# Layer 1 inputs in the order q, z, kv; S4, scaled tables and the second sequence's turned x1 through DRAM

## The chip, the core and the metric

The kernel runs on one core of a Trainium2 chip. The metric is the device time of one execution in microseconds (us). The core's engines work side by side, each through its own list of instructions in order: PE (TensorE) multiplies matrices into PSUM banks, DVE (VectorE), ACT (ScalarE) and POOL (GpSimd) work on elements, and SP (SyncE) issues nearly all DMA transfers, one after the other. An instruction that waits holds up all that stand behind it on its engine.

## What is computed

Two sequences, p of 1024 tokens and s of 512, run through two layers of width 1024. Layer 0 mixes by pooling and a gated recurrence; layer 1 is attention with eight query heads, two key/value heads, RMS norm and rotary positions (rope) on q and k, and a gate from z:

```python
def odd_mixer(x, w_in, q_norm_g, k_norm_g, w_out):
    proj = x @ w_in
    q, k, v, z = jnp.split(proj, IN1_SPLIT_POINTS, axis=-1)
    q = rms_norm(q.reshape(B, T, ATTN_HEADS, HEAD_DIM), q_norm_g)
    k = rms_norm(k.reshape(B, T, KV_HEADS, HEAD_DIM), k_norm_g)
    ...
    q = apply_axial_rope(q, cos, sin)
    k = apply_axial_rope(k, cos, sin)
    o = blocked_attention(q, k, v)
    return (o * jax.nn.silu(z)) @ w_out

for layer in range(DEPTH):
    ...
    x = layer_norm(ALPHA * x + mix, ln_g[layer], ln_b[layer])
```

## The kernel before

**Numbers.** Every matrix operand is split into a high part (`h`, rounded to the matmul type) and a low part (`l`, what is left); a product is three matmuls: high x high, low x high, high x low. ACT or POOL makes the high part (L88, L85), DVE the low part (L91). A `unit` is a 128x512 block of weights: one load, one high, one low.

**Stages.** Layer 0's projections run to about 170 us, its heads to 620, its output and the layer norm ("mid") to 752. `layer1_in` then makes the inputs of layer 1 until 1119, and attention and output follow. In mid, `mid_pair` turns the rows of x1 for p on PE and makes the six operands A11, A12, A22, S1, S2, S3 from them.

**The products of p.** `PRODUCTS` names seven products that replace eight block products, in the order P1 (A11), P2 (A12), P6 (S2), P5 (S1), P3 (S4), P7 (S3), P4 (A22). S4 = A12 - S2 is a seventh operand, which `last_sum` makes after P2 of kv, from the split parts: sum, sum, difference, high, low (L975 to L977). The sums of weights that the products need are made in layer 0 by `weight_sums`, a generator that the projections advance (two steps per group), and stored to DRAM. `gathered` adds each product's bank on DVE (L1094) to tiles u2 and u4 or to one of two c tiles; a finished block goes to `finish`, which is `kv_done`, `q_done` or, in `z_pair`, the gate. Only then is the bank free; there are five banks, `mm` (two) and `me` (three), used in turn. A kv tile takes 12 matmuls of 256 columns per bank, a q or z tile 12 of 512.

**Order.** For p: kv, z, q. `feed` lists the units in this order, and `next_units` keeps up to eight prepared ahead. The first eight are made during mid, in tiles of their own. Then comes s: its four blocks of x1 are loaded, turned (L903), split and used for kv (`kvs`), q (`qs`) and z; its units come from `wunit`, high part on POOL. A scheduler orders the instructions of each engine from the program's order and its own estimates of durations.

**Rope.** `rope` takes squares on ACT (L996), a small op on DVE (L997), pow on POOL (L999), the product with the cos table (L1001, on POOL for p, on DVE for s), one product with the sin table per head on DVE (L1006), and the add on POOL (L1007). For q a further DVE op (L1155) scales the result of pow into `rq`; for k the result scales the rows on DVE (L1137). PE turns the rows (L1159 for q, into Tqp or Tqs; L1138 for k, into kTkp or kTks), ACT copies q out of PSUM, and a DMA stores it to qd. `rope_consts` loads cos, sin and the gains and multiplies the tables on DVE (L1016), anew for k of p, q of p and both of s.

Of the kernel before, what the change touches and what calls it, by code (L numbers as in the profile page):

```python
# [56 lines left out]
class Kern:  # L57
    def __init__(self, ctx, tc, a):
# [906 lines left out]
    def last_sum(self):  # L965

        nc = self.nc
        tags = [f"x{p}{k}0" for k in range(4) for p in "hl"]
        at = {"h": tags[0::2], "l": tags[1::2]}
        parts = {x: [self.x0p.tile([P, 512], F32R, tag=t, name=f"S4{x}{k}") for k, t in enumerate(at[x])] for x in "hl"}  # L970
        for k in range(4):
            (ah, al), (sh, sl) = (tuple(x[k // 2][:, k % 2, :] for x in self.A[b]) for b in ("A12", "S2"))
            a, b = self.raw(f"s4a{k}"), self.raw(f"s4b{k}")
            add = nc.gpsimd if k % 2 else nc.vector
            add.tensor_tensor(out=a, in0=ah.bitcast(F32), in1=al.bitcast(F32), op=ALU.add)  # L975
# [13 lines left out]
    def rope(self, ps, nh, n, tabs, t1, t2, name, mul):  # L989
# [7 lines left out]
        nc.vector.tensor_scalar(ss[:, 0:nh], ss[:, 0:nh], 1.0 / DH, RMS_EPS, ALU.mult, ALU.add)  # L997
# [1 line left out]
        nc.gpsimd.tensor_tensor(out=rs[:, 0:nh], in0=ss[:, 0:nh], in1=self.mhalf[:, 0:nh], op=ALU.pow)  # L999
# [1 line left out]
        mul.tensor_tensor(out=t1[:, 0:W].rearrange("p (h f) -> p h f", f=P), in0=ps.rearrange("p (h f) -> p h f", f=P),  # L1001
                                in1=ct[:, n:n + 1, :].to_broadcast([P, nh, P]), op=ALU.mult)
# [566 lines left out]
```

## Time and profile before

| what | us |
|---|---|
| three runs | 1573.17, 1573.67, 1574.72 |
| median | 1573.67 |
| the profiled execution, its own time | 1565.18 |
| its span in the trace | 1563.2 |

The span is what the trace covers; the views count from its start. The profiled execution is a run of its own, 8.5 us under the median of the other three. In the prediction's fences a group row reads: line, engine, operation, output and inputs by the program's names, shapes, count | busy us, mean ns of one | idle time before them and who ended it.

### The profile page before, as it was taken

How to read it: one execution, taken by the hardware profiler on the slowest of the kernel's cores; microseconds unless marked ns; L12 is line 12 of the kernel's file. 1: busy time of each engine (PE TensorE's matmuls, PEld its weight loads, DVE VectorE, ACT ScalarE, POOL GpSimd, SP SyncE). 2: the span in 40 equal slices, each digit the busy share in tenths (PEclk: the TensorE clock that was granted, in tenths of full speed). 3: DMA queues.
4: the chain of work that ended last, by engine and by line, in shares of the span. 5: the costliest groups of instructions: out<-in, count | busy, mean ns of one | idle time of the engine just before them, and what ended most of it. 6: DMA issues, size and time to landing. Idle time of an engine off the chain costs nothing.

```text
span 1563.2 us, 21698 instructions
## 1 busy us (share of the span) xinstructions
PE 1474.5 (94%) x7214; PEld 1211.3 (77%) x7214; DVE 1077.7 (69%) x2062; ACT 722.2 (46%) x1628; POOL 727.9 (47%) x726
## 2 busy tenths in 40 slices
PE   9989998989987989999889999899999999999997
PEld 7767886878776778778778877677778888888786
DVE  5672256587767978868795378766577777777775
ACT  3222354555554655345244343412675555555651
POOL 5441244254375563539740046855444444544642
PEclk9999999999997999999999999999999999999999
DMA  9962343234535646544435444444340111111211
GB/s 329 371 219 64 116 115 90 92 109 127 158 106 162 189 149 196 162 136 156 135 120 173 140 161 122 112 125 142 108 148 28 55 54 55 55 49 60 80 63 54
DMA packets 150144, 198.58 MB, mean 127 GB/s; under 512 B 12032, under 2 KB 77824, under 8 KB 150032
## 3 DMA queue, kind: packets, MB, share of 16 engines
q1 hardware_dynamic: 150032, 197.19, 39.8%
q8 instruction: 57, 0.93, 0.3%
q14 instruction: 55, 0.45, 0.1%
HBM read 139.43 MB, written 57.72 MB: 126 GB/s over the span
## 4 chain that ended last, share of the span: by engine, by line
PE 59%; DVE 20%; DMA 9%; ACT 4%; issue 4%; POOL 2%; SPq 1%; DVEq 0%; ACTq 0%; POOLq 0%
PE Sp L98 6%; PE Op L98 5%; PE o1p L98 5%; PE tp L98 4%; PE ptp L1357 3%; PE o1s L98 3%; PE o0p L98 3%; PE zp L98 3%; PE qs L98 3%; PE ts L98 2%; PE z L98 2%; DVE t1qp L1006 1%; PE o0s L98 1%; PE Ss L98 1%; PE z4P L98 1%
## 5 line engine op out<-in xcount | busy, mean ns | idle before, releaser
L1335 POOL TENSOR_SCALAR prp<-prp,smp 128x1024 f32<-128x1024 f32 x64 | 72.6, 1134 | 124.7 <-DVE smp L1334 114.1
L88 ACT CAST pwp<-ptp 128x512 fp32r<-128x512 f32 x128 | 74.8, 584 | 95.8 <-PE ptp L1357 95.6
L98 PE MATMUL Op<-pwp,Vhp 128*128 128x512 f32 x256 | 108.9, 425 | 0.0
L91 DVE TENSOR_TENSOR pwp<-ptp,pwp 128x512 fp32r<-128x512 f32 x128 | 87.1, 682 | 21.3 <-ACT pwp L88 21.3
L1330 ACT ACTIVATE prp<-Sp,nbp,rqp 128x1024 f32<-128x1024 f32 (+1 forms) x68 | 78.7, 1158 | 20.5 <-DVE nbp L1327 14.0
L1322 DVE TENSOR_REDUCE nbp<-Sp 128x1 f32<-128x1024 f32 (+1 forms) x68 | 78.3, 1153 | 9.7 <-PE Sp L98 9.7
L1357 PE MATMUL ptp<-idn,prp 128*128 128x128 f32 x512 | 77.4, 273 | 4.1 <-ACT zs L1260 3.2
L1357 PEld LDWEIGHTS ptp<-idn,prp 128*128 128x128 f32 x512 | 64.0, 141 | 22.2 <-POOL prp L1335 4.7
L1001 POOL TENSOR_TENSOR t0qp<-cq,rt0qp 128x512 f32<-128x512 f32 x8 | 10.7, 1339 | 107.9 <-DVE cq L1094 100.5
L98 PEld LDWEIGHTS Op<-pwp,Vhp 128*128 128x128 f32 x256 | 48.3, 189 | 7.0
L98 PE MATMUL o0p<-wo0h,ah0p 128*128 128x512 f32 x128 | 51.1, 400 | 0.4 <-ACT wo0h L88 0.4
L98 PE MATMUL o0p<-wo0l,ah0p 128*128 128x512 f32 x128 | 51.0, 400 | 0.0
L98 PE MATMUL o0p<-wo0h,al0p 128*128 128x512 f32 x128 | 50.9, 398 | 0.0
L98 PE MATMUL tp<-wt_l,xhp 128*128 128x512 f32 x128 | 50.3, 397 | 0.0
L98 PE MATMUL tp<-wt_h,xlp 128*128 128x512 f32 x128 | 50.3, 396 | 0.0
L98 PE MATMUL Op<-pwp,Vlp 128*128 128x512 f32 x128 | 50.1, 391 | 0.0
L98 PE MATMUL tp<-wt_h,xhp 128*128 128x512 f32 x128 | 49.8, 402 | 0.0
L658 DVE SCALAR_TENSOR_TENSOR Usp<-Usp,decbp 128x130 f32<-128x130 f32 x48 | 23.7, 495 | 27.7 <-ACT Usp L623 27.2
L98 PE MATMUL Sp<-Khp,qhp 128*128 128x512 f32 x128 | 42.4, 408 | 0.0
L1335 POOL TENSOR_SCALAR prs<-prs,sms 128x512 f32<-128x512 f32 x32 | 24.3, 761 | 36.1 <-DVE sms L1334 23.8
L98 PE MATMUL Sp<-Klp,qhp 128*128 128x512 f32 x128 | 41.0, 396 | 0.0
L98 PE MATMUL Sp<-Khp,qlp 128*128 128x512 f32 x128 | 40.8, 395 | 0.0
(1181 smaller groups left out, 5251.3 us busy)
## 6 DMA issues: line engine op xcount, KB each, us to landing
wt_r<-w0t SPq DMA_DIRECT2D x16, 256.0 KB, 4.1
xrp<-xT_p SPq DMA_DIRECT2D x16, 256.0 KB, 5.1
srq<-w1q SPq DMA_DIRECT2D x16, 256.0 KB, 5.4
xrs<-xT_s SPq DMA_DIRECT2D x16, 256.0 KB, 5.1
sum_q<-srq SPq DMA_DIRECT2D x16, 256.0 KB, 5.1
srz<-w1z SPq DMA_DIRECT2D x16, 256.0 KB, 4.2
sum_z<-srz SPq DMA_DIRECT2D x16, 256.0 KB, 2.3
wp<-rd_p SPq DMA_DIRECT2D x16, 256.0 KB, 5.3
```

The source lines that it names most:

```text
L88: self.nc.scalar.copy(out, in_)
L91: self.nc.vector.tensor_tensor(out=out, in0=in_, in1=hi.bitcast(F32), op=ALU.subtract)
L98: self.nc.tensor.matmul(out, lhsT=lhsT, rhs=rhs, start=start, stop=stop)
L658: nc.vector.scalar_tensor_tensor(out=U[:, i, :], in0=U[:, i + o, :], scalar=dec[:, 4 * d + h, n:n + 1], in1=U[:, i, :], op0=ALU.mult, op1= ...
L1001: mul.tensor_tensor(out=t1[:, 0:W].rearrange("p (h f) -> p h f", f=P), in0=ps.rearrange("p (h f) -> p h f", f=P), in1=ct[:, n:n + 1, :].to ...
L1006: nc.vector.tensor_tensor(out=v(t2[:, c]), in0=v(ps[:, c])[:, :, ::-1, :], in1=v(st[:, n, :]), op=ALU.mult)
L1322: nc.vector.tensor_reduce(out=nb[:, i:i + 1], in_=b, op=ALU.max, axis=AX.X, negate=True)
L1330: nc.scalar.activation(pr[:, i * W:(i + 1) * W], b, AF.Exp, bias=nb[:, 0:1], scale=rq, accum_out=sm[:, i:i + 1])
L1335: nc.gpsimd.tensor_scalar(pr, pr, sm, 0.0, ALU.mult, ALU.add)
L1357: nc.tensor.transpose(pt[:, h * P:(h + 1) * P], prs[h][:, c * P:(c + 1) * P], self.idn)
```

## The change

1. **Order.** For p the stages run q, z, kv. `feed` and `weight_sums` follow; the first eight units are those of P1 and P2 of q.
2. **S4.** `mid_pair` computes S4 in one DVE instruction from the unsplit S2 and the turned A12 and stores it to DRAM; `last_sum` loads it and splits it.
3. **Tables.** `weight_sums` ends with two more steps: cos and sin are multiplied with the four gains, once, and stored; `rope_tables` loads them.
4. **Rope.** The cos product is on DVE for p too; the sin product is two instructions for all heads; q's pow writes `rq` itself (the small op adds 128 times the epsilon, which includes the scale); k's scale moves from DVE to ACT.
5. **x1 of s.** After each of the four `z_pair`s `turn_second` loads one block of x1, turns and splits it, and stores the parts to DRAM; after P1 and after P2 of kv `load_second` loads one half of them back, into the tiles that A11 and A12 leave.
6. **High parts.** For the units of s (and half of the output's) they are made on ACT, no longer on POOL.
7. `z_pair` takes its sums from the u tiles in a rotation of four, not two.

```diff
+        s4 = hp.tile([P, 512], F32, tag="xbp", name=f"s4{i}", bufs=2)
+        nc.vector.scalar_tensor_tensor(out=s4, in0=s2, scalar=-1.0, in1=p12, op0=ALU.mult, op1=ALU.add)
+        self.load(self.s4d[:, :, c], v(s4))
...
-            add.tensor_tensor(out=a, in0=ah.bitcast(F32), in1=al.bitcast(F32), op=ALU.add)
-            add.tensor_tensor(out=b, in0=sh.bitcast(F32), in1=sl.bitcast(F32), op=ALU.add)
-            add.tensor_tensor(out=a, in0=a, in1=b, op=ALU.subtract)
+            raw = self.raw(f"s4{k}")
+            self.load(raw, self.s4d[:, k, :])
...
-        mul.tensor_tensor(out=t1[:, 0:W].rearrange("p (h f) -> p h f", f=P), in0=ps.rearrange("p (h f) -> p h f", f=P),
+        nc.vector.tensor_tensor(out=t1[:, 0:W].rearrange("p (h f) -> p h f", f=P), in0=ps.rearrange("p (h f) -> p h f", f=P),
                                 in1=ct[:, n:n + 1, :].to_broadcast([P, nh, P]), op=ALU.mult)
-        for h in range(nh):
-            c = slice(h * P, (h + 1) * P)
-            v = lambda x: x.rearrange("p (a b f) -> p a b f", b=2, f=32)
-            nc.vector.tensor_tensor(out=v(t2[:, c]), in0=v(ps[:, c])[:, :, ::-1, :], in1=v(st[:, n, :]), op=ALU.mult)
+        v = lambda x, b: x.rearrange("p (h a b f) -> p h a b f", a=2, b=2, f=32)[:, :, :, b, :]
+        for b in range(2):
+            nc.vector.tensor_tensor(out=v(t2[:, 0:W], b), in0=v(ps, 1 - b),
+                                    in1=v(st[:, n, :], b).to_broadcast([P, nh, 2, 32]), op=ALU.mult)
...
+        for h in range(2):
+            for i, n in enumerate(("cos", "sin")):
...
+                for w in range(2):
...
+                    nc.vector.tensor_tensor(out=o, in0=t, in1=g[:, 2 * w + i:2 * w + i + 1, :].to_broadcast([P, 4, P]), op=ALU.mult)
+                    self.load(self.tabd[w][i][:, ns, :], o)
...
-            nc.vector.tensor_scalar(t1[:, c], t1[:, c], rs[:, h:h + 1], None, ALU.mult)
+            nc.scalar.activation(t1[:, c], t1[:, c], AF.Copy, scale=rs[:, h:h + 1])
...
-        nc.vector.tensor_scalar(self.rq[s][:, n, 4 * piece:4 * piece + 4], rs, QK_SCALE, None, ALU.mult)
...
-        self.token_products("kv", 2, 256, u, kv_done, self.last_sum)
+        self.next_units(0)
         tabs = table(0, "qp")
+        self.token_products("q", 1, 512, u, q_done, lambda j: j == 1 and self.last_sum())
         for b in range(0, 8, 2):
             self.z_pair(b, u)
...
-        self.token_products("q", 1, 512, u, q_done)
+            self.turn_second(b // 2)
+        tabs = table(1, "kp")
+        self.token_products("kv", 2, 256, u, kv_done, lambda j: j < 2 and self.load_second(j))
...
+        self.hi_w = self.hi_act
...
+    def turn_second(self, i):
+
+        y = [self.tp.tile([P, 512], F32, tag="c", name=f"y1{i}{half}", bufs=2) for half in range(2)]
+        for half in range(2):
+            self.load(y[half], self.x1["s"][i][:, 512 * half:512 * half + 512])
+            pt = self.turned(y[half], 0, "mx", f"x1t{i}{half}")
+            h, l = (self.tp.tile([P, 512], F32R, tag="t", name=f"x1{x}{i}{half}", bufs=4) for x in "hl")
+            self.hi_act(h, pt)
+            self.lo_dve(l, pt, h)
+            for d, x in zip(self.x1t, (h, l)):
+                self.load(d[half][:, :, i * P:(i + 1) * P], x.bitcast(F32).rearrange("p (k t) -> p k t", t=P))
+
+    def load_second(self, half):
+        for j in (2 * half, 2 * half + 1):
+            for x, d, X in zip("hl", self.x1t, (self.XH, self.XL)):
+                X[2][j] = self.x1p.tile([P, 2, 512], F32R, tag=f"x1{x}2{j}", name=f"x1{x}2{j}")
+                self.load(X[2][j].bitcast(F32), d[half][:, 2 * (j % 2):2 * (j % 2) + 2, :])
```

How this moves the instructions is shown at three places; the scheduler decides them. Numbers behind names are tile numbers and differ between the kernels, as do line numbers (L1094 is L1109 after the change, L91 is L95, L1006 is L1011, L98 is L102).

First, DVE at the start of layer 1, from the first add that needs P2's bank. Before it is kv (ckv a c tile, kvP2i and kvP6i the banks, s4a and s4b the two sums for S4, rt0kp the cos table):

```order
L1094 TENSOR_TENSOR ckv_7818<-u_7721,kvP2i_7805 128x256
L1094 TENSOR_TENSOR ckv_7853<-u_7722,kvP2i_7840 128x256
L997 TENSOR_SCALAR sskp_7821<-sskp_7821 128x2
L1094 TENSOR_TENSOR u_7722<-u_7722,kvP6i_8007 128x256
L997 TENSOR_SCALAR sskp_7856<-sskp_7856 128x2
L975 TENSOR_TENSOR s4a_7953<-A12h_6723,A12l_6725 128x512
L976 TENSOR_TENSOR s4b_7954<-S2h_6727,S2l_6729 128x512
L1094 TENSOR_TENSOR u_7721<-u_7721,kvP6i_7993 128x256
L1016 TENSOR_TENSOR rt0kp<-rt0kp,rgkp 128x1024
L977 TENSOR_TENSOR s4a_7953<-s4a_7953,s4b_7954 128x512
L1016 TENSOR_TENSOR rt1kp<-rt1kp,rgkp 128x1024
```

After the change the same place is q (t0qp the cos product, t1qp the sin product, wlq the low part of a unit, S_ that of S4):

```order
L1109 TENSOR_TENSOR cq_7875<-u_7770,qP2i_7862 128x512
L1007 TENSOR_TENSOR t0qp_7877<-cq_7875,rt0qp 128x512
L1004 TENSOR_SCALAR ssqp_7879<-ssqp_7879 128x4
L1011 TENSOR_TENSOR t1qp_7878<-cq_7875,rt1qp 128x8x32 x2
L1109 TENSOR_TENSOR cq_7910<-u_7771,qP2i_7897 128x512
L95 TENSOR_TENSOR wlq_7839<-q0t_r,whq_7838 128x512
L1007 TENSOR_TENSOR t0qp_7912<-cq_7910,rt0qp 128x512
L95 TENSOR_TENSOR wlq_7845<-q1t_r,whq_7844 128x512
L95 TENSOR_TENSOR wlq_7851<-q2t_r,whq_7850 128x512
L1004 TENSOR_SCALAR ssqp_7914<-ssqp_7914 128x4
L1011 TENSOR_TENSOR t1qp_7913<-cq_7910,rt1qp 128x8x32 x2
L95 TENSOR_TENSOR wlq_7857<-q3t_r,whq_7856 128x512
```

The sums for S4 and the table products are gone from between the adds; the cos products have come in.

Second, DVE where P2 of kv now begins (kr are k's products with cos and sin):

```order
L1109 TENSOR_TENSOR ckv_9515<-u_7770,kvP2i_9502 128x256
L1007 TENSOR_TENSOR kr_9517<-ckv_9515,rt0kp 128x256
L1109 TENSOR_TENSOR ckv_9550<-u_7771,kvP2i_9537 128x256
L1001 TENSOR_SCALAR sskp_9518<-sskp_9518 128x2
L1011 TENSOR_TENSOR kr_9517<-ckv_9515,rt1kp 128x4x32 x2
L1007 TENSOR_TENSOR kr_9552<-ckv_9550,rt0kp 128x256
L1001 TENSOR_SCALAR sskp_9553<-sskp_9553 128x2
L1011 TENSOR_TENSOR kr_9552<-ckv_9550,rt1kp 128x4x32 x2
```

An add and its row's products now follow each other, and no scale of kr stands among them.

Third, PE where the keys and values of s begin. Before (x1t is a turned block of x1, kvs the bank, Tqp a turned row of q):

```order
L903 MATMUL x1t_10001<-idn,y_9999 128x128 x4
L1159 MATMUL Tqp_9697<-idn,t0qp_9680 128x128 x4
L98 MATMUL kvs_10136<-wkv_h,x1h_9991 128x512
L98 MATMUL kvs_10136<-wkv_l,x1h_9991 128x512
L1159 MATMUL Tqp_9736<-idn,t0qp_9719 128x128 x4
L98 MATMUL kvs_10136<-wkv_h,x1l_9995 128x512
```

and after, behind the last matmul of P4 of kv:

```order
L102 MATMUL kvP4i_10024<-whkv_9724,A22l_6779 128x256
L102 MATMUL kvs_10125<-wkv_h,x1h_9482 128x512
L102 MATMUL kvs_10125<-wkv_l,x1h_9482 128x512
L102 MATMUL kvs_10125<-wkv_h,x1l_9484 128x512
L102 MATMUL kvs_10125<-wkv_h,x1h_9482 128x512
```

The turns of x1 have gone to the z stage, and the rows of q that were still to be turned here have gone with q to the front.

More of the change, by code (lines that the diff above doesn't have):

```diff
@@ L309, in layer0 @@
                         if piece or gi:
-                            for _ in range(2):
+                            for _ in range(4 if piece and gi == len(groups) - 1 else 2):
                                 next(presums, None)
@@ L965, in last_sum @@
     def last_sum(self):
[L967 to L970, printed above, removed]
+        self.S4 = [], []
         for k in range(4):
[L972 to L975, printed above, removed]
-            add.tensor_tensor(out=b, in0=sh.bitcast(F32), in1=sl.bitcast(F32), op=ALU.add)
-            add.tensor_tensor(out=a, in0=a, in1=b, op=ALU.subtract)
-            self.hi_act(parts["h"][k], a)
-            self.lo_dve(parts["l"][k], a, parts["h"][k])
-        self.S4 = parts["h"], parts["l"]
+            h, l = (self.x0p.tile([P, 512], F32R, tag=f"x{'hl'[k % 2]}{2 * j + k // 2}0", name=f"S4{j}{k}") for j in range(2))
+            raw = self.raw(f"s4{k}")
+            self.load(raw, self.s4d[:, k, :])
+            self.hi_act(h, raw)
+            self.lo_dve(l, raw, h)
+            self.S4[0].append(h)
+            self.S4[1].append(l)
     def a_part(self, b, k):
@@ L1124, in token_products, with k_rows @@
                 self.gathered(prod, i, ps, u, W, finish, f"{name}{i}")
[L1125 to L1128 removed]
+            if after:
+                after(j)
+    def k_rows(self, s, g, i, src, tabs, t):
         nc = self.nc
@@ L1217, in layer1_in @@
         c4.close()
         tp = self.tp = ctx.enter_context(self.tc.tile_pool(name="t1p", bufs=1, reuse_waits="tile"))
-        tabs = [[t[:, 4 * w:4 * w + 4, :] for t in both] for both in [[tp.tile([P, 8, P], F32, tag=f"rt{i}", name=f"rts{i}") for i in range(2)]] for w in range(2)]
-        for w in range(2):
-            self.rope_consts(w, tp.tile([P, 2, P], F32, tag="rg", name=f"rgs{w}"), tabs[w], 4)
-        self.XH, self.XL = ({2: [self.x1p.tile([P, 2, 512], F32R, tag=f"x1{x}2{j}", name=f"x1{x}2{j}") for j in range(4)]} for x in "hl")
@@ L1224, in layer1_in @@
-        for i in range(4):
-            c = slice(i * P, (i + 1) * P)
-            y = self.x1p.tile([P, D], F32, tag=f"x1{'hl'[i % 2]}0{i // 2}", name=f"y1{i}")
-            self.load(y, self.x1[s][i])
-            for half in range(2):
-                pt = self.turned(y, half, "mx", f"x1t{i}{half}")
-                for j in range(2):
-                    xh, xl = (x[2][2 * half + j][:, :, c] for x in (self.XH, self.XL))
-                    pv = pt[:, 256 * j:256 * j + 256].rearrange("p (k t) -> p k t", t=P)
-                    self.hi_act(xh, pv)
-                    self.lo_dve(xl, pv, xh)
+        both = [tp.tile([P, 8, P], F32, tag=f"rt{i}", name=f"rts{i}") for i in range(2)]
@@ L1235, in layer1_in @@
+        tabs = [self.rope_tables(w, [t[:, 4 * w:4 * w + 4, :] for t in both], 4) for w in range(2)]
+        self.hi_w = self.hi_act
         self.kv_places(s, iter([f"x{x}{k}0" for k in range(4) for x in "hl"]))
```

68 lines of the change are left out of this document (37 added, 31 removed).

## The prediction

> **What bounds the kernel now.** First the page's head: which engine is nearly always busy.
>
> ```profile
> span 1563.2 us, 21698 instructions
> PE 1474.5 (94%) x7214; PEld 1211.3 (77%) x7214; DVE 1077.7 (69%) x2062; ACT 722.2 (46%) x1628; POOL 727.9 (47%) x726
> ```
>
> PE is busy for 94% of the span, but its ends are modelled, so "busy" hides stalls shorter than a matmul's modelled tail. The change touches the input of layer 1, so the second view is the table of windows over that stretch, cut where the chain of waits and the timeline show the parts to begin: keys/values of the first sequence (752), z (814), q (890), the second sequence's turning and keys/values (977), its q (1019), its z with the first scores (1072). The last row is this whole stretch.
>
> ```profile
> core 0: us, PE busy (x) PEld busy (x) DVE busy (x) ACT busy (x) POOL busy (x), PEclk, DMA share, GB/s
> 752.00:814.00 62.00, 49.81 (x359) 46.52 (x358) 52.26 (x109) 23.55 (x68) 32.42 (x30) 0.94 0.42 134
> 814.00:890.00 76.00, 76.00 (x334) 61.49 (x333) 44.18 (x82) 32.24 (x64) 7.05 (x9) 1.00 0.55 162
> 890.00:977.00 87.00, 83.82 (x373) 67.37 (x372) 60.96 (x114) 33.15 (x119) 39.28 (x33) 0.98 0.44 137
> 977.00:1019.00 42.00, 35.21 (x169) 27.46 (x167) 32.51 (x68) 19.23 (x82) 32.41 (x31) 0.92 0.45 125
> 1019.00:1072.00 53.00, 49.94 (x211) 38.84 (x210) 32.68 (x78) 9.99 (x53) 29.60 (x31) 0.94 0.35 103
> 1072.00:1120.00 48.00, 42.31 (x185) 33.67 (x184) 29.28 (x63) 27.38 (x67) 26.61 (x29) 0.96 0.54 162
> 752.00:1119.50 367.50, 336.58 (x1618) 274.85 (x1616) 251.68 (x510) 145.54 (x449) 167.08 (x161) 0.96 0.46 139
> ```
>
> Columns: stretch, its length, busy time of PE, weight load, DVE, ACT and POOL, the granted PE clock, DMA share and rate. In the z window PE has no idle time and full clock. In the first window it idles for 62.00 - 49.81 = 12.2 us, in 977:1019 for 6.8, in 1072:1120 for 5.7, and the clock is below one in just these windows. Over the stretch the idle time is 367.5 - 336.58 = 30.9 us; the clock loss, (1 - clock) x length added up over the six windows, is about 14 us.
>
> The third view, the chain of waits, gives PE's undisturbed pace and shows what starts the first window late.
>
> ```profile
> 765.55 5.59 DMA rt0kp<-cos
> ...
> 803.86 1.42 PE kvP4i L98 x12
> ...
> 850.86 19.53 PE z4P L98 x84
> ...
> 991.73 0.45 PE x1t L903 x4
> ```
>
> z4P: 84 matmuls of 512 columns in 19.53 us, 0.2325 us each. kvP4i: 12 of 256 columns in 1.42, 0.118 each. A group of four transposes: 0.45 at most. From these I make a floor for the stretch: kv of the first sequence 336 x 0.118 = 40; z and q 336 x 0.2325 = 78 each; the second sequence's kv 96, q 192, z 144 and 21 early score matmuls, 453 x 0.2325 = 105; some 38 groups of transposes, about 17. Together 319 of 367.5, so **about 48 us of excess**: 18 in 752:890 (138 - 40 - 78 - 2), 16 in 890:1019, 6 in 1019:1072, 8 after. That is all that the change can win here.
>
> The fourth view, PE's waits in these windows (engine, what waited, for whom: us, times, longest), names the causes.
>
> ```profile
> PE kvP5i L98 <- DVE ckv L1094: 3.6, 1, 3.6
> ...
> PE qP4i L98 <- DVE u L1094: 2.0, 1, 2.0
> PE Tqp L1159 <- POOL t0qp L1007: 1.2, 1, 1.2
> ...
> PE kvs L98 <- DVE x1l L91: 2.8, 3, 1.7
> PE x1t L903 <- DVE x1l L91: 2.1, 2, 2.0
> ...
> PE qs L98 <- POOL wq_h L85: 1.4, 1, 1.4
> ...
> PE ptp L1357 <- ACT zs L1260: 3.2, 1, 3.2
> ```
>
> The first window waits for DVE, which is late with the adds that empty the banks. The turn of the second sequence waits for its own low parts, one group after the other, and its kv for the last of them.
>
> **The change, part by part.** *The first window (order q, z, kv).* In the chain the tables land at 765.55 + 5.59 = 771.1 and must then be multiplied on DVE; DVE meanwhile forms S4. A kv bank lasts PE 12 x 0.118 = 1.4 us, five banks 7 us, so a DVE that is ten us late stops PE. A q bank lasts 12 x 0.2325 = 2.8 us, five banks 14 us. With q first, P2's third bank is full at 752 + 48 x 0.2325 + 3 x 2.8 = 771.6, and is wanted again by P6's third tile at 780. The tables, now only loaded, still stand behind the four stores of x_s on SP's queue, so they land near 771 again; P2's third add needs the c tile of the first row, some 6 us later (rope, turn, store): 777 against 780. P6's own four units stand behind the tables on SP, and PE wants them at 752 + 96 x 0.2325 = 774.3, just when they can be landed and split. I charge 1.5 us, bounded by 0 and by today's wait of 3.6 us for ckv.
>
> DVE's load decides whether q then keeps PE's pace.
>
> ```profile
> L1006 DVE TENSOR_TENSOR t1qp<-cq,rt1qp 128x128 f32<-128x128 f32 x32 | 15.9, 532 | 1.9 <-ACT t1qp L996 1.9
> L1006 DVE TENSOR_TENSOR krs<-kvs,rts 128x128 f32<-128x128 f32 x8 | 1.8, 277 | 0.0
> L1155 DVE TENSOR_SCALAR rqp<-rsqp 128x4 f32<-128x4 f32 x16 | 14.0, 877 | 3.5 <-POOL rsqp L999 3.5
> L997 DVE TENSOR_SCALAR ssqp<-ssqp 128x4 f32<-128x4 f32 x16 | 4.6, 289 | 0.0
> L1094 DVE TENSOR_TENSOR u<-u,qP7i 128x512 f32<-128x512 f32 x8 | 5.2, 674 | 0.0
> L1001 DVE TENSOR_TENSOR tqs<-qs,rts 128x512 f32<-128x512 f32 x8 | 5.5, 683 | 0.0
> L1001 DVE TENSOR_TENSOR krs<-kvs,rts 128x256 f32<-128x256 f32 x4 | 1.6, 414 | 0.0
> L91 DVE TENSOR_TENSOR wlq<-q2t_r,whq 128x512 fp32r<-128x512 f32 x4 | 2.7, 683 | 0.0
> ```
>
> Columns: line, engine, operation, tiles, shape, count | busy us, mean ns of one | idle before. A q row on DVE costs today 4 x 0.532 + 0.289 + 0.877 = 3.3 us. Afterwards: cos product 0.683 (the second sequence's row), two sin products of 128x256 at 0.414, the small scalar op 0.289, no scale: 1.8 us at the quiet price. But the first sequence's rope reads two tiles beside a busy POOL, and there the same sin product takes 532 ns instead of 277, a factor 1.92; the three products at that factor make 2.9 + 0.3 = 3.2 us. I take 2.5, half way, because POOL keeps pow and the add of a row but loses its cos product, 16 x 1.34 = 21 us:
>
> ```profile
> L1001 POOL TENSOR_TENSOR t0qp<-cq,rt0qp 128x512 f32<-128x512 f32 x8 | 10.7, 1339 | 107.9 <-DVE cq L1094 100.5
> ```
>
> DVE's sum for q: 28 low parts at 0.683 = 19, 28 adds at 0.674 = 19, 16 rows x 2.5 = 40, four S4 low parts 2.7: 81 us (70 to 92) against PE's 78 + 16 groups, 85. It fits, narrowly. ACT's part of q is unchanged. What remains is the ring of two c tiles, released by the stores of q:
>
> ```profile
> DVE cq L1094 <- DMA qd_p<-cq: 7.5, 2, 4.2
> ```
>
> DVE stood 7.5 us for them, and PE 2.0 + 1.2 for DVE and POOL; these stay. With 1.5 for the start and 2 for DVE's tightness: **excess of q 7** (5 to 14).
>
> [...]
>
> *z* has no waits now. It gains the second x1's turn: eight groups of transposes among 336 matmuls (the same groups leave 977:1019), and on DVE eight low parts of 128x512, against 44 of 76 us busy. Hidden; it adds waits on SP (x1 loads wait for the two c tiles, x1t stores for ACT and DVE, with z units queued behind both; but these are loaded up to eight units, 8 x 2.8 = 22 us, ahead). **Excess 1** (0 to 5).
>
> *kv, now last.*
>
> ```profile
> L91 DVE TENSOR_TENSOR S4l<-s4a,S4h 128x512 fp32r<-128x512 f32 x4 | 4.2, 1048 | 0.0
> L1094 DVE TENSOR_TENSOR u<-u,kvP7i 128x256 f32<-128x256 f32 x8 | 3.0, 410 | 0.0
> L91 DVE TENSOR_TENSOR Klp<-kTkp,Khp 128x128 fp32r<-128x128 f32 x16 | 4.2, 280 | 0.5 <-ACT Khp L88 0.5
> L975 DVE TENSOR_TENSOR s4a<-A12h,A12l 128x512 f32<-128x512 f32 x2 | 1.9, 945 | 0.0
> L1137 DVE TENSOR_SCALAR kr<-kr,rskp 128x128 f32<-128x128 f32 x16 | 8.2, 554 | 0.0
> ```
>
> S4's two sums, difference and low part (the rows of about 0.9 and 1.05, some 9 us on DVE), the table products and L1137 (8.2 us) leave DVE. What stays: 14 low parts 9.6, 28 adds at 0.41 = 11.5, eight rows (0.414 + 2 x 0.277 + 0.25) = 9.7, Klp 16 x 0.28 = 4.5, Vlp eight at about 0.42 = 3.4: 39 us against PE's 42 (47 if rope costs the loaded price). L1137 goes to ACT, which is busy 32.2 of 76 us or less in these windows and hides it. SP's queue now meets eight loads of x1 that wait for PE's last use of A11 and A12; behind them stand the last kv units and the eight wkv units. Those are wanted 15 us later, and a 512 KB load landed in 5.7 us:
>
> ```profile
> rt1kp<-sin SPq DMA_DIRECT2D x1, 512.0 KB, 5.7
> ```
>
> and this one had a twin of its size beside it, so eight take 4 x 5.7 = 23 us at the worst, with 30 us of kv left to hide it. **Excess 5** of today's 18 with z (2 to 10).
>
> *Second sequence.* Turn, copies and low parts leave 977:1019; the loads of whole halves replace them. The waits for x1l (2.8 and 2.1), the clock at 0.92 and half of the transposes' jam go: kvs **2** (1 to 6) of today's 16 with q. In q(s) only the wait for POOL's high part goes (1.4): **5** of 6. In z(s) the rope's tail shortens by the four-head sin product, but the 3.2 us for zs stay: **6** of 8.
>
> *Elsewhere.* The tables' eight products now run on DVE in layer 0, near 124 to 138 us, where gates already wait a little:
>
> ```profile
> L1016 DVE TENSOR_TENSOR rts<-rts,rgs 128x512 f32<-128x512 f32 x4 | 3.6, 910 | 0.5 <-DMA rgs<-g 0.5
> ...
> PE ctsws L468 <- DVE ggs L463: 0.2, 1, 0.2
> ```
>
> 8 x 0.91 = 7.3 us of DVE; between 0, if they fall into gaps, and all 7.3 ahead of the gates; I take 1, nearer to the present wait of 0.2. S4's four subtractions and stores are one instruction each, against three of 0.7 to 0.95 today, but stand ahead of the split of S1 to S3: 0.5. wo1's eight high parts go to ACT in attention: spread over the attention, with ACT at 46% of the span: nothing.
>
> Sum of excess after: 7 + 1 + 5 + 2 + 5 + 6 = 26 against 48, less 1.5 elsewhere: **saving about 21 us**, against the profiled run's own 1565.2 us (span 1563.2 and 2.0 around it) that is 1544. That run stands 8.5 us under the median of the runs, 1573.67; the same saving there gives **1552.5**.
>
> **Rivals.** *A: rope at the loaded price.* If the cos product meets POOL each time, q's DVE sum is 92 against 85 and kv's 47 against 42: excess 14 + 1 + 10 + 2 + 5 + 6 = 38, saving 48 - 38 - 1.5 = 9, 1565. For it: 532 against 277. Against: those 532 were taken beside the POOL cos product that starts on the same tile, which is gone.
>
> *B: slower.* The same contention on all of DVE's work, low parts too, since POOL's add now falls between them. With factor f on 70 and 39: excess 70f - 85 + 39f - 42 + 14. It equals 46.5 at f = 1.46; from there on the kernel is slower; at 1.6 the excess is 61 and the time about 1589. Against it: adds of 674 and low parts of 683 in q beside a POOL that is busy 39.28 of 87 us, and still within 10 ns of each other: neither shows any contention.
>
> *C: no difference.* The waits are replaced one for one: SP, issuing in order, holds the last kv and the wkv units behind the x1 loads (half of their 23 us uncovered, 11), and q's start waits for tables and units behind the x_s stores (10, if the third row's add comes at 790). Together 21 us: 1573. For it: one queue carries all; against it: units run eight ahead.
>
> *D: more is won.* If all of PE's waits in q, kv and q(s) go, the excess is about 10: saving 37, 1537.
>
> **How the numbers follow.** A measurement of this kernel tells about 0.2%, 3.1 us, from no change. Forecast (saving 13 to 32) 0.60; A and like losses (4 to 13) 0.19; D 0.10; C 0.04; B 0.07. Faster 0.89, same 0.04, slower 0.07. The range leaves out B, C and the edges of A and D: 1534 to 1567.
>
> **What would show it.** Right: 752 to the end of q without a wait of over 2 us for DVE; kv under 46 us; kvs beginning with no x1 transposes among it; windows' clock at 0.98 or more. Wrong: cos and sin products of the first sequence over 1 us each (A); low parts over 0.9 us in q (B); kv or wkv units waiting for DMA behind x1 loads, or q's P6 for the tables (C).

## The result, and the profile after

The changed kernel takes 1530.13 us (median of 4 runs, 1525.20 to 1536.39) against 1574.20 for the kernel before: a ratio of 0.9723, 95% interval 0.9684 to 0.9761. Forecast were 1552.5 and a range of 1534 to 1567. The sign is right, but 44 us were gained where 21 were forecast, and the time lies outside the range. The profiled execution is the slowest of the four, 1536.39 us with a span of 1534.7.

The windows of the changed kernel, cut at its stages: q (762), z (850), kv (935), kv of the second sequence (978.3), its q (1001.5), its z (1050.5), and the whole stretch.

```profile
core 0: us, PE busy (x) PEld busy (x) DVE busy (x) ACT busy (x) POOL busy (x), PEclk, DMA share, GB/s
762.00:850.00 88.00, 84.14 (x372) 67.12 (x371) 64.64 (x113) 41.53 (x136) 37.47 (x30) 0.98 0.51 164
850.00:935.00 85.00, 84.57 (x392) 68.45 (x391) 53.59 (x88) 42.75 (x103) 15.19 (x12) 1.00 0.77 235
935.00:978.30 43.30, 42.47 (x354) 41.84 (x353) 31.37 (x84) 22.18 (x69) 7.67 (x10) 1.00 0.69 231
978.30:1001.50 23.20, 23.20 (x107) 18.77 (x106) 12.07 (x34) 13.05 (x47) 11.70 (x13) 1.00 0.44 128
1001.50:1050.50 49.00, 49.00 (x230) 39.88 (x229) 26.02 (x59) 25.28 (x97) 17.07 (x16) 1.00 0.39 120
1050.50:1089.70 39.20, 39.20 (x174) 31.70 (x173) 21.49 (x42) 30.86 (x60) 11.98 (x9) 1.00 0.56 167
762.10:1089.70 327.60, 322.48 (x1617) 267.66 (x1617) 209.10 (x417) 175.66 (x508) 100.96 (x88) 0.99 0.58 183
```

Here and below, kvs, q(s) and z(s) are the second sequence's keys and values, q and z. From q's start on, PE is idle for 88.00 - 84.14 = 3.9 us in the first window, below 1 in each of the next two, and not at all in the three windows of the second sequence, where the clock is at 1.00. Before, these three had 6.8, 3.1 and 5.7 us of idle time and clocks of 0.92 to 0.96. The stretch takes 327.6 us instead of 367.5: 39.9 us less, against some 22 in the prediction's sum. PE's waits in the same windows, where nothing is listed after 978:

```profile
PE qP6i L102 <- DVE u L1109: 2.2, 1, 2.2
PE qP6i L102 <- ACT whq L92: 1.0, 1, 1.0
PE qP6i L102 <- DVE wlq L95: 0.7, 1, 0.7
...
PE x1t L907 <- DMA y<-x_s: 0.3, 1, 0.3
...
PE kTkp L1153 <- ACT kr L1152: 0.5, 1, 0.5
PE kTkp L1153 <- DVE Klp L95: 0.4, 1, 0.4
```

What is left stands where the prediction charged 1.5 us, at P6 of q. SP's timeline of the changed kernel (start, length, instruction) points to why it is more:

```profile
765.04 11.48 SPq L86 DMA_DIRECT2D x_s<-xr0s  x5
778.60 0.32 SPq L86 DMA_DIRECT2D rt0qp<-tab  x1
779.27 0.32 SPq L86 DMA_DIRECT2D rt1qp<-tab  x1
779.68 0.38 SPq L86 DMA_DIRECT2D q0t_r<-sum_q  x1
```

SP stands for 11.48 us at the stores of x_s. Only then go the tables, at 778.60, and P6's units. The first of these is issued at 779.68, and PE wants it landed and split at 784.3 (762 + 96 x 0.2325). DVE's first add into a c tile also waits 3.5 us for these stores. No experiment moved them, so this cause is not shown.

The groups of p's q rows after the change, to compare with L1006, L1155 and L997 before:

```profile
L1007 DVE TENSOR_TENSOR t0qp<-cq,rt0qp 128x512 f32<-128x512 f32 x8 | 6.5, 816 | 2.3 <-DMA rt0qp<-tab 2.0
L1007 DVE TENSOR_TENSOR t0qp<-u,rt0qp 128x512 f32<-128x512 f32 x8 | 5.4, 680 | 1.2 <-POOL t0qp L1013 1.2
L1011 DVE TENSOR_TENSOR t1qp<-cq,rt1qp 128x256 f32<-128x256 f32 x16 | 6.0, 416 | 1.5 <-DMA rt1qp<-tab 1.5
L1011 DVE TENSOR_TENSOR t1qp<-u,rt1qp 128x256 f32<-128x256 f32 x16 | 8.3, 552 | 0.0
L1004 DVE TENSOR_SCALAR ssqp<-ssqp 128x4 f32<-128x4 f32 x16 | 5.6, 353 | 0.6 <-ACT t1qp L999 0.6
```

On average a q row costs DVE 0.75 + 2 x 0.48 + 0.35 = 2.1 us (taken were 2.5 between 1.8 and 3.2), and POOL's part no longer has a product.

Two more things are read off all profiles. The span before the stretch is 752.0 us in the first profile of before and 762.1 in that of after, but 749.6 to 755.9 in the fifteen others, with or without the tables there. Five of these differ from the changed kernel in layer 1 alone and reach the stretch at 750.5 to 755.9. So the 10 us belong to that execution, not to the change. And the part after the stretch is 443.7 before, 445.0 after, and 441.8 to 446.6 in the others.

### The profile page after: what moved, and what is told of

Same layout as the page of the kernel before. It is cut to its first block, busy times and chain, and to the rows that moved or that the text cites. A ratio compares the mean times of both kernels' runs of the same rounds, so it can differ in the third digit from the quotient of the medians.

```text
span 1534.7 us, 21703 instructions
## 1 busy us (share of the span) xinstructions
PE 1470.8 (96%) x7214; PEld 1212.1 (79%) x7214; DVE 1034.3 (67%) x1980; ACT 755.4 (49%) x1692; POOL 658.2 (43%) x648
## 4 chain that ended last, share of the span: by engine, by line
PE 61%; DVE 17%; DMA 10%; ACT 4%; issue 4%; POOL 2%; SPq 0%; DVEq 0%; ACTq 0%; POOLq 0%
PE Sp L102 6%; PE o1p L102 5%; PE Op L102 5%; PE tp L102 5%; PE ptp L1380 3%; PE o1s L102 3%; PE qs L102 3%; PE z L102 3%; PE o0p L102 2%; PE ts L102 2%; PE zp L102 2%; PE xap L102 1%; PE xbp L102 1%; PE kvs L102 1%; DMA wp<-rd_p 1%
## 5 line engine op out<-in xcount | busy, mean ns | idle before, releaser
L102 PE MATMUL Op<-pwp,Vhp 128*128 128x512 f32 x256 | 109.0, 426 | 0.6 <-DVE pwp L95 0.6
L95 DVE TENSOR_TENSOR pwp<-ptp,pwp 128x512 fp32r<-128x512 f32 x128 | 87.3, 682 | 23.3 <-ACT pwp L92 23.1
L102 PEld LDWEIGHTS Op<-pwp,Vhp 128*128 128x128 f32 x256 | 48.3, 189 | 8.0 <-DVE pwp L95 1.0
L102 PE MATMUL o0p<-wo0h,ah0p 128*128 128x512 f32 x128 | 51.5, 405 | 2.7 <-DVE xr0p L844 1.9
L102 PE MATMUL o0p<-wo0h,al0p 128*128 128x512 f32 x128 | 52.0, 406 | 0.0
L102 PE MATMUL o0p<-wo0l,ah0p 128*128 128x512 f32 x128 | 51.7, 406 | 0.1
L102 PE MATMUL tp<-wt_h,xlp 128*128 128x512 f32 x128 | 50.5, 398 | 0.0
L1005 POOL TENSOR_TENSOR rskp<-sskp,mhalf 128x2 f32<-128x2 f32 x8 | 7.1, 883 | 100.6 <-DVE sskp L1001 100.6
L102 PE MATMUL Op<-pwp,Vlp 128*128 128x512 f32 x128 | 50.1, 391 | 0.0
L102 PE MATMUL tp<-wt_l,xhp 128*128 128x512 f32 x128 | 50.0, 395 | 0.0
L102 PE MATMUL tp<-wt_h,xhp 128*128 128x512 f32 x128 | 49.8, 401 | 0.0
L102 PE MATMUL Sp<-Khp,qhp 128*128 128x512 f32 x128 | 42.2, 406 | 0.0
L102 PE MATMUL Sp<-Klp,qhp 128*128 128x512 f32 x128 | 41.1, 397 | 0.0
L102 PE MATMUL Sp<-Khp,qlp 128*128 128x512 f32 x128 | 40.8, 395 | 0.0
L102 PE MATMUL o1p<-wo,ah1p 128*128 128x512 f32 x128 | 40.7, 398 | 0.0
```

The lines of the kernel that those rows point to most:

```text
L95: self.nc.vector.tensor_tensor(out=out, in0=in_, in1=hi.bitcast(F32), op=ALU.subtract)
L102: self.nc.tensor.matmul(out, lhsT=lhsT, rhs=rhs, start=start, stop=stop)
```

## The experiments

Each kernel was profiled and timed together with the kernel before; the ratio is to that kernel's times of the same occasion, so medians of different rows are compared less well than ratios. "Stretch" is read from PE's timeline, from the first matmul of layer 1's input to the first ptp transpose; it is free of what layer 0 does in one execution or another.

| kernel | median us | ratio to before, interval | stretch |
|---|---|---|---|
| before, first profile | 1574.20 | | 367.5 |
| before, again | 1570.59 | 1.0002, 0.9988 to 1.0015 | 370.0 |
| changed | 1530.13 | 0.9723, 0.9684 to 0.9761 | 327.6 |
| changed, old order | 1527.28 | 0.9732, 0.9706 to 0.9757 | 327.4 |
| changed, old turn | 1531.56 | 0.9756, 0.9734 to 0.9778 | 331.8 |
| changed, high parts on POOL | 1524.90 | 0.9720, 0.9692 to 0.9748 | 331.1 |
| changed, old S4 | 1533.97 | 0.9780, 0.9755 to 0.9805 | 332.6 |
| changed, old tables | 1528.09 | 0.9742, 0.9723 to 0.9761 | 330.4 |
| changed, old rope | 1541.14 | 0.9828, 0.9808 to 0.9848 | 342.4 |
| changed, old order, S4, tables | 1543.65 | 0.9840, 0.9820 to 0.9859 | 342.5 |
| before, new rope | 1546.47 | 0.9865, 0.9838 to 0.9892 | 350.4 |
| before, new order, S4, tables | 1541.88 | 0.9834, 0.9809 to 0.9859 | 344.8 |
| before, new turn and high parts | 1567.37 | 0.9993, 0.9980 to 1.0006 | 365.9 |
| changed, cos product on POOL | 1531.91 | 0.9760, 0.9732 to 0.9788 | 333.9 |
| changed, old scales | 1528.74 | 0.9751, 0.9701 to 0.9801 | 328.0 |
| changed, old order, tables | 1541.15 | 0.9831, 0.9788 to 0.9874 | 342.7 |
| changed, old order, S4 | 1530.90 | 0.9758, 0.9712 to 0.9804 | 332.6 |

Two profiles of the same kernel, the first two rows, differ by 2.5 us in the stretch, so a single loss of 3 to 5 us is little more than that. By their intervals six kernels stand apart from the changed one: old rope; old order and tables, with or without S4; and the three on top of before. Point 7 of the change, the rotation of four in `z_pair`, stayed in every edit and was not tried by itself.

**The kernel before, again.** No edit.

> The kernel before, unchanged, profiled again. Theory 1 (the first profile of before was a lucky execution: 1565.2 against a median of 1574): its stretch from the first matmul of layer 1's input to the first ptp transpose again lasts 367 us, and the 8 to 9 us more lie in layer 0, where the clock of the head stage is lower. Rival (the stalls of layer 1's input cost more in usual runs than in that profile): the stretch itself lasts 372 us or more, and layer 0 is as long as in the first profile (752 us).

The stretch is 370.0 us, the span 1565.0. Neither 367 nor 372: the two profiles lie 2.5 us apart there, with layer 0 at 751.2. Ten runs reached from 1566.9 to 1572.8. So the first profile lay at the fast end of the runs, and the median of three that the prediction added its 8.5 us for, 1573.67, at the slow end; where the runs differ was not settled by this profile.

**The old order alone.**

```diff
-        order = [("q", k, b) for _, _, b in self.PRODUCTS for k in range(4)]
+        order = [("kv", k, b) for _, _, b in self.PRODUCTS for k in range(2)]
...
-        self.token_products("q", 1, 512, u, q_done, lambda j: j == 1 and self.last_sum())
+        self.token_products("kv", 2, 256, u, kv_done, lambda j: j == 1 and self.last_sum())
```

> The changed kernel with p's stages in the old order kv, z, q, all else as changed. Theory (kv at the start meets a DVE that is late, and its five banks hold only 7 us): the kv stage takes 8 to 14 us more than the 43 it takes in last place, q and z the same; in all 6 to 14 us slower than the changed kernel, near 1540. Rival (the S4 sums, the table products and k's scale made kv slow, not its place): kv takes at most 46 us, total within 4 us of the changed kernel, near 1532.

kv takes 51.0 us instead of 43.3: 7.7 more, just under the theory's 8 to 14. But q, now in third place, takes 82.9 instead of 88.6, and the stretch is the same to 0.2 us, so the 6 to 14 us in all are not there. The start is late by about as much whichever stage meets it: with kv in front PE's waits there are 3.6 us for ckv and 0.9 for u, with q in front 3.9 in all.

**The old turn.** The loop of before, in its place behind the last stage of p, instead of `turn_second` and `load_second`.

```diff
-            self.turn_second(b // 2)
...
+            y = self.x1p.tile([P, D], F32, tag=f"x1{'hl'[i % 2]}0{i // 2}", name=f"y1{i}")
+            self.load(y, self.x1[s][i])
```

> The changed kernel with the second sequence's x1 loaded, turned and split after the last stage of p, as before. Theory (the turn's chain of transposes, high and low parts holds PE at that place): kvs and the turn take 35 us or more against 23, PE waits 4 us or more for x1l, total 8 to 14 us slower, near 1541. Rival (before, the jam came from q's tail on POOL and DVE, which is no longer beside it): at most 29 us there, total up to 5 us slower.

The turn and kvs take 963.7 to 1002.2, 38 us against 23, as the theory says. But PE's waits for x1l are 1.8 us, not 4 or more. Of the 15 us, 5.6 come back because the transposes are no longer in z (81.2 for 84.6) and kv (41.1 for 43.3), and another 6 because q(s) already starts among them, at 993.8. The stretch is only 4.2 us longer, and the ratio, 0.9756, lies within the changed kernel's interval. In size the rival was nearer.

**High parts on POOL.**

```diff
-        self.hi_w = self.hi_act
```

> The changed kernel with the high parts of the second sequence's units (and of half the output's) on POOL again. Theory of the prediction (they cost one wait of 1.4 us): q and z of the second sequence lose 1 to 3 us, total near 1532. Rival (POOL's high parts made nearly all of the 14 us that these two stages lost): they lose 8 us or more, total near 1540.

q(s) takes 48.6 us (48.8 with ACT), z(s) 40.2 (39.1), together 0.9 more, where the theory had 1 to 3. Of the 3.5 us in the stretch 2.0 lie in p's q, which this edit does not touch, and the time did not grow. POOL's high parts did not make the losses of these stages.

**S4, the tables, the rope, singly.** S4 as in the diff's minus lines; the tables with `rope_consts`; rope with the three functions of before.

```diff
-        self.S4 = [], []
+            add.tensor_tensor(out=a, in0=ah.bitcast(F32), in1=al.bitcast(F32), op=ALU.add)
...
-            self.load(t, self.tabd[which][i][:, 0:nt, :])
+            nc.vector.tensor_tensor(out=t, in0=t, in1=g[:, i:i + 1, :].to_broadcast([P, nt, P]), op=ALU.mult)
...
-        self.rope(src, 4, n, tabs, t1, t2, nm, self.rq[s][:, n, 4 * piece:4 * piece + 4])
+        rs = self.rope(src, 4, n, tabs, t1, t2, nm, mul)
+        nc.vector.tensor_scalar(self.rq[s][:, n, 4 * piece:4 * piece + 4], rs, QK_SCALE, None, ALU.mult)
```

> The changed kernel with S4 formed again after P2 (of q now) from the split parts, two of the four on POOL. Theory (with q first the five banks hold 14 us, which covers 9 us more on DVE): the stretch from q's first matmul to the first ptp transpose grows by at most 5 us from 327.6, total near 1533. Rival (S4 is what made the start late): the stretch grows by 8 to 12 us, total near 1540.

> The changed kernel with the rope tables multiplied with the gains anew in layer 1 (DVE, 128x1024 twice for q, twice for k, four 128x512 for the second sequence). Theory (about 9 us of DVE in three stages that keep slack): the stretch grows by at most 4 us, total near 1532. Rival (the wait for the multiplied table at the start of q holds the banks): PE waits 4 us or more in P6 of q, total near 1537.

> The changed kernel with rope, its scale for q and k's scale as before (cos product of p on POOL, sin product per head, the scale of rq and of kr on DVE). Theory now (the rope on POOL and the two scales made the jam at q's end that spread into all that followed): the stretch grows by 12 us or more, total 1542 to 1555. Rival (rope is one of several equal parts): it grows by 3 to 7 us, total near 1535.

S4 costs 5.0 us of the stretch, at the edge of the theory's 5. The tables cost 2.8, within its 4. PE then waits 4.7 us for a high part of P6, as the rival says, but with the tables as changed the same wait is also up to 3.2 us, so at most part of it is theirs. The old rope costs 14.8, more than the theory's 12, and its waits name it:

```profile
PE Tqp L1170 <- POOL t0qp L1009: 12.4, 12, 4.0
PE qP6i L102 <- ACT whq L92: 1.6, 1, 1.6
PE qP6i L102 <- DVE wlq L95: 1.3, 1, 1.3
```

PE waits twelve times for POOL, 12.4 us: 4.3 in q, 8.1 in z, none in the second sequence. With q in front, z takes the tail of q's rows.

**Old order, S4 and tables together, then in pairs.**

> The changed kernel with the old order, S4 and the tables as before, all three at once; rope, turn and high parts stay changed. Theory (late DVE work at the start and banks that hold 7 us belong together: the order counts only with S4 and the tables in their old place): kv takes 58 us or more (51 with the order alone), PE waits over 6 us for DVE there, total 8 to 14 us over the changed kernel, near 1540. Rival (each part counts by itself): the losses add up from the single runs, under 6 us together.

> The changed kernel with the old order and the tables multiplied in layer 1; S4 stays as changed. Singly they cost 0 and 3 us; with S4 all three cost 15. Theory (the tables meet q's tail: with q last the second sequence's table is loaded and multiplied behind q's last rope, and k's rows of the second sequence wait): kv takes 51 to 53 us, q(s) 52 or more with a wait of PE for krs, stretch 334 to 337. Rival (S4 is the other half): stretch at most 331.

> The changed kernel with the old order and S4 formed in layer 1; stored tables stay. Theory (S4's 9 us on DVE meet banks of 7 us): kv takes 56 us or more against 51 with the order alone, q(s) stays at 48, stretch 333 to 337. Rival (only S4 and tables together overrun the banks): kv at most 53, stretch at most 331.

Edits as above, joined. Together they cost 14.9 us, where the single costs add up to 7.6, and kv takes 58.5, as the first theory says. The pair of order and tables has all of it (15.1): its theory was right on q(s), but had kv at 51 to 53 and the stretch at 334 to 337. The pair of order and S4 costs 5.0, as S4 alone. kv takes 55.6 and the stretch 332.6, just under its theory's 56 and 333 and over its rival's 53 and 331. The windows of order and tables show both places, kv in the first and the second sequence's q in the fifth:

```profile
core 0: us, PE busy (x) PEld busy (x) DVE busy (x) ACT busy (x) POOL busy (x), PEclk, DMA share, GB/s
754.00:810.00 56.00, 46.92 (x346) 45.37 (x345) 43.92 (x101) 24.46 (x75) 21.71 (x20) 0.91 0.52 169
810.00:890.00 80.00, 80.00 (x369) 65.24 (x368) 46.02 (x81) 38.37 (x79) 6.03 (x7) 1.00 0.69 218
890.00:973.00 83.00, 83.00 (x383) 67.73 (x382) 57.38 (x100) 39.24 (x131) 27.89 (x22) 1.00 0.58 184
973.00:998.30 25.30, 25.30 (x126) 20.74 (x125) 16.61 (x33) 15.72 (x65) 15.93 (x14) 1.00 0.58 164
998.30:1054.00 55.70, 51.31 (x221) 39.54 (x220) 30.57 (x67) 24.89 (x88) 16.51 (x16) 0.97 0.44 137
1054.00:1096.60 42.60, 40.18 (x182) 32.35 (x180) 22.42 (x47) 31.32 (x71) 16.92 (x13) 1.00 0.50 157
```

and PE's waits there:

```profile
PE kvP2i L102 <- ACT u L1109: 2.9, 1, 2.9
PE kvP5i L102 <- DVE u L1101: 2.6, 1, 2.6
PE kvP6i L102 <- DVE ckv L1101: 1.9, 1, 1.9
PE qs L102 <- DVE krs L1011: 1.4, 1, 1.4
PE qs L102 <- DVE wq_l L95: 1.0, 2, 0.7
```

kv takes 59.3 us against 51.0 with the order alone. At the start the table has to land and be multiplied while banks of 7 us wait; DVE stands 2.9 us for it:

```profile
DVE rt0kp L1022 <- DMA rt0kp<-cos: 2.9, 1, 2.9
```

q(s) takes 55.8 against 48.2: PE is idle for 55.70 - 51.31 = 4.4 us of its window, the clock is 0.97, and the named waits are for krs and wq_l. The first of these is the kv rows' sin product with the second sequence's table. That table can be loaded only when q's last row has released the tile (988.9); its load is issued at 993.2, the second set of gains at 1000.7, and the first product with k's table starts at 1007.6, 9.3 us after q(s) began.

**Single parts on top of the kernel before.** The same edits the other way round.

> The kernel before with the new rope alone (cos product on DVE, two sin products, no scale of rq, k's scale on ACT). Theory (the parts stand in for each other: what one leaves jammed another clears): the stretch, 367 to 370 us before, falls by less than the 14.8 us that undoing it in the changed kernel cost or by about as much, to 352 to 360, and the waits of q(s) and z(s) for DVE and POOL fall below 2 us. Rival (rope alone does most, since q's tail on POOL is the root of all later waits): to 345 or less.

> The kernel before with the new order, S4 and stored tables alone; old rope, turn and high parts. Theory: the stretch falls by about 15 us as undoing them in the changed kernel cost, to 352 to 357; waits for POOL's t0qp stay, 8 us or more, since rope is the old one. Rival (with q in front its jam is absorbed by z, so that little of the rest remains): to 345 or less.

> The kernel before with the turn of x1 in the z stage (through DRAM) and the high parts on ACT alone. Theory (undone singly in the changed kernel they cost 4 us each; in the kernel before the same place carried q's tail as well, and its excess was some 13 us): the stretch falls by 10 to 16 us, to 353 to 359. Rival (they are worth the sum of the single costs): by 6 to 9 us, to 360 or more.

Rope alone gains 17 to 20 us of the stretch (theory: 352 to 360; it is 350.4), and no wait of q(s) or z(s) is left. Order, S4 and tables gain 23 to 25: 344.8, the rival's side, though the waits for t0qp stay, 12.0 us. Turn and high parts gain 2 to 4 us of the stretch, less than theory and rival say, and in time nothing that shows (ratio 0.9993). This third one shows best where a gain can go. The turn and kvs fall from 42 us to 31; then PE and DVE wait in the same place for something else. PE's waits, and DVE's, from 975 on:

```profile
PE qs L102 <- DVE krs L1010: 8.3, 1, 8.3
PE qs L102 <- DVE wq_l L95: 2.6, 1, 2.6
PE kvs L102 <- DVE wkv_l L95: 1.9, 3, 0.9
```

and DVE's:

```profile
DVE rts L1020 <- DMA rgs<-g: 5.6, 1, 5.6
DVE rts L1020 <- DMA rts<-cos: 2.2, 1, 2.2
```

DVE stands 2.2 us for the table of the second sequence, which could not be fetched before 1008, since q's rope was at work with the tile until then. It stands 5.6 for the second set of gains, which go into the one tile of the first set and are fetched at 1021.65, after that set's last use. The first product with k's table starts at 1028.40. Before, the same delay lay under the turn of x1 (DVE's and SP's timelines: q's last use of the sin table, the loads, the first product):

```profile
1006.46 0.28 DVE L1006 TENSOR_TENSOR t1qp<-u,rt1qp 128x128 f32<-128x128 f32 x1
1009.00 0.40 SPq L82 DMA_DIRECT2D rts<-cos  x1
1018.13 0.35 SPq L82 DMA_DIRECT2D rgs<-g  x1
1025.79 0.74 DVE L1001 TENSOR_TENSOR krs<-kvs,rts 128x256 f32<-128x256 f32 x2
```

The wait took the place of the one removed: 11 us were won, 8.3 came back at once.

**Rope in halves.**

```diff
-        nc.vector.tensor_tensor(out=t1[:, 0:W]...
+        (mul or nc.vector).tensor_tensor(out=t1[:, 0:W]...
```

> The changed kernel with p's cos product (q and k) on POOL again, but without the old scales and with the two-part sin products. Theory (POOL's 21 us for q's cos products are what costs, PE waiting for t0qp): of the 14.8 us of the whole old rope 9 or more return, stretch 337 or more. Rival (the scales L1155 and L1137 on DVE, 22 us together, cost more): 4 us or less return, stretch under 332. By contention, DVE's sin product for c tiles, 416 ns now, goes to 600 ns or more in either case.

```diff
-            nc.scalar.activation(t1[:, c], t1[:, c], AF.Copy, scale=rs[:, h:h + 1])
+            nc.vector.tensor_scalar(t1[:, c], t1[:, c], rs[:, h:h + 1], None, ALU.mult)
```

(and the scale of rq as above)

> The changed kernel with the two scales on DVE again (rq's own op per q row, kr's per k head); cos products stay on DVE, sin products in two parts. The cos product on POOL alone returned 6 us of the 15 that the whole old rope cost. Theory (the rest are the scales: some 14 us for rq, 8 for kr on DVE, and q's DVE sum goes from about 70 to 84 against PE's 84): stretch 334 to 338, total near 1537. Rival (the parts of rope need each other, as DVE has room for 14 us): stretch at most 331.

The cos product on POOL costs 6.3 us, between its theory (9 or more) and its rival (4 or less). The scales on DVE cost 0.4, as their rival says. Together with the sin product per head they cost 14.8. PE's waits for POOL's t0qp go the same way: 4.5 us and 1.5 us in the halves, 12.4 in the whole. So DVE's scales cost nothing where POOL has no product. Where the other 8 us of the whole come from is open: the sin product per head was not tried by itself, nor in pairs with the others. With the cos product on POOL, DVE's sin product takes longer on average:

```profile
L1011 DVE TENSOR_TENSOR t1qp<-cq,rt1qp 128x256 f32<-128x256 f32 x16 | 8.2, 552 | 2.8 <-DMA rt1qp<-tab 2.8
L1011 DVE TENSOR_TENSOR t1qp<-u,rt1qp 128x256 f32<-128x256 f32 x16 | 12.6, 822 | 0.0
```

These are 552 and 822 ns against 416 and 552 in the changed kernel; the c tiles' rows stay short of the 600 that was written down. But such a mean hides two durations. The tile view gives shortest, median and longest in ns (first two lines before, then the changed kernel, then cos on POOL):

```profile
L1006 DVE TENSOR_TENSOR t1qp<-cq,rt1qp x32: 275/278/1377, 905.1 to 966.4; 128x128 f32<-128x128 f32 x32
L1155 DVE TENSOR_SCALAR rqp<-rsqp x16: 156/1236/1262, 907.9 to 1007.9; 128x4 f32<-128x4 f32 x16
L1011 DVE TENSOR_TENSOR t1qp<-u,rt1qp x16: 411/412/1533, 842.9 to 867.2; 128x256 f32<-128x256 f32 x16
L1011 DVE TENSOR_TENSOR t1qp<-u,rt1qp x16: 410/412/1517, 831.5 to 858.1; 128x256 f32<-128x256 f32 x16
```

Of 32 sin products of p's q rows two are long in the changed kernel (1528 and 1533 ns), eight with the cos product on POOL (1479 to 1525), none with the old scales; the others take 409 to 427. Each long one began while an add or a product of 128x512 was running on POOL and ended 0.28 to 0.29 us after it, so it waited for the whole rest of it. POOL's pow beside them (most ran beside one) cost nothing.

## Why the prediction was wrong

**Right**: what bounds the stretch (PE, held by late DVE and POOL work); the floor of 319 us (its terms add up to 318), which the changed kernel comes within 9 us of; z at 1 us of excess (measured 84.6 against 78.1 and 13 groups of transposes, 5.7: 0.8); layer 0's tables and attention at too little to see; the DVE price of a rope row, 2.1 where 2.5 was taken, though the 2.5 came from a wrong factor (see rival A).

**Right in size, by luck in part**: q at 7 (88.5 - 78.1 - 9 groups, 4.0 = 6.4). The start took 3.9 where 1.5 was charged, and the waits of 2.0 and 1.2 us that were to stay are gone. The signs named for being right nearly all came (the longest wait for DVE up to the end of q is 2.2 us where 2 was the bound, kv takes 43.3, no x1 transposes stand at kvs, the clock is at 0.98 or more), but none of them watches q(s) and z(s), where most of the error lies.

**Wrong, the main step**: the excess kept for kv, kvs, q(s) and z(s), "5", "2", "5 of 6" and "6 of 8", 18 us. By the same floor the chip shows 1.9 (43.3 - 39.6 - 1.8 of transposes), 0 (23.2 - 22.3 - 0.9), 0.2 (49.0 - 44.6 - 3.5 of transposes - 0.7 of scores) and 0.1 (39.1 against 164 matmuls and two groups, 39.0): 16 us less. The prediction read each wait of the trace as the property of its stage and of the engine named last, and let it go only where the change touched that very instruction: in q(s) "only the wait for POOL's high part goes". But the run with these high parts on POOL again leaves q(s) at 48.6 us, and the pair of old order and old tables brings it back to 55.8 without touching a high part. Those waits were lateness handed down: q's rope tail released the table late, the kv rows of the second sequence came late to their table, their banks were free late. A sign of it stood in the trace of before, in the window of the turn and kvs, and the prediction does not list it:

```profile
PE Tqp L1159 <- POOL t0qp L1007: 1.4, 1, 1.4
```

All 17 profiles fall in line (timelines of DVE and PE). In five the first product with the second sequence's table starts 9.0 to 16.5 us after q(s)' first matmul: both of before, turn and high parts alone, and old order with tables, with and without S4. There q(s) takes 53.9 to 62.3 us from its first matmul to its last. In the other twelve that product starts at most 1.0 us after it, and q(s) takes 47.9 to 50.9. PE's wait for zs at the end of z(s), which was to "stay" with 3.2 us, goes the same way: 2.5 to 3.3 us in the five, 1.1 in two of the twelve (old order alone, old order with S4), none in the other ten. So one lateness stood behind waits that the prediction priced stage by stage. Why kv needs 3 us less than the 5 kept for it was not tried.

Undone in the changed kernel, the parts come near the whole of 39.9 to 42.4 us: rope 14.8, order with S4 and tables 14.9, turn 4.2, high parts 3.5, together 37.4. None of them, alone, brings all back.

**A reading that was wrong.** "The clock is below one in just these windows" leaves out two windows: it was 0.98 in 890:977 and 0.94 in 1019:1072.

**The bank argument** for the order was right in kind and wrong in what it earns: kv alone loses 7.7 us in front, and q gains 5.7 behind. The order earns its share only together with the tables.

**Rival A** was too dear: means in the changed kernel were 0.68 to 0.82 us for cos and 0.42 to 0.55 for sin, not over 1. The factor 1.92, and with it 2.5 for a row, was made from a mean of two durations: before, 46 of the 64 sin products took 0.28 to 0.34 us and 18 took 0.69 to 1.38, 12 of these beside POOL's cos product. The Trainium skill, page "SBUF — State Buffer", section "Who interferes with whom", says that a DVE instruction with two SBUF inputs contends with a GpSimd (POOL) one that reads SBUF, that the ports they share are "an exclusive lock", and that a `tensor_scalar` can contend too, in a mode that uses two ports. The traces agree: each long sin product ends a fixed time after POOL's instruction, 0.13 to 0.15 us before the change, and of the 16 scales L1155 eleven were held in the same way (0.93 to 1.26 us against 0.16). So the price of a row hangs on how often an instruction of DVE begins behind one of POOL's. What the held ones took above the shortest adds up, in the rope of p's q on DVE, to 28 us before, to 6 after the change and to 13 with the cos product on POOL. **Rival B** did not occur: the adds from PSUM stayed at 0.67 to 0.69, and of q's 24 low parts (its units' and S4's) four were held behind POOL's add (1.1 to 1.6 us), while the others took 0.68 to 0.69. **Rival C's** wait at q's start is there with 3.9 us instead of 10. **D**, "saving 37, 1537", at a chance of 0.10, is nearest to what happened; the time is 7 us below even that.

**The reference**: 21 us were taken off both the profiled run and the median. The stretch accounts for 39.9 us by the two profiles and 42.4 by the second one of before; medians give 44. The rest is within what runs of one kernel differ by: 1565 to 1575 for nearly all of before, 1525 to 1536 after.

## What to carry to other kernels

A wait in a trace can belong to a chain that was late long before the stage in which it is seen. Before keeping it in a forecast, follow the engine waited for back to what it did until then, and ask whether the change shortens that. Parts that hide one another's lateness are not worth the sum of their single effects. Undo them in pairs (order and tables: 0 and 3 us alone, 15 together) and apply them singly to the old kernel (turn of x1 with the high parts: 2 to 4 us of the stretch, nothing that shows in the time) before calling a part useless or good. Look at shortest, median and longest before taking a mean for a price: 0.55 us was 0.41 and, now and then, 1.53. And compare stages between profiles rather than whole spans where a span moves by 10 us from run to run.

## What the runs showed of the hardware

A DVE instruction of the rope of p's q, or a low part there, took its own time or was held by POOL. In the profiles of before, after, cos on POOL and old scales 65 held ones were followed. Each began while an add or product of 128x512 (four times a high part) was running on POOL, and each ended a fixed time after it: 0.02 to 0.03 us for a 128x4 scalar op, 0.13 to 0.15 for a sin product of 128x128, 0.28 to 0.29 for one of 128x256, 0.55 for a cos product or low part of 128x512. That is some 0.13 us less than each takes unheld (0.16, 0.28, 0.41, 0.68). Among the rope's own products, small ops and scales one short one, a sin product of before, began 0.06 us after a POOL product and was not held; adds with one input in PSUM never were (0.67 to 0.69 us in q).

So a 128x4 scale on DVE took 0.16 us, or up to 1.26, more than an add of 128x512. With the old scales on DVE eleven of sixteen were held, 11 us of DVE in all, and the stretch grew by 0.4 us all the same. Layer 0 and mid, which differ by at most the eight table products, S4's subtractions with their stores and the order of the weights' sums, took from 749.6 to 762.1 us in the profiles.
